# A decoder trunk's mixer: the delta rule's chain moved ahead of the stick-breaking attention, its small products joined, and the output projection begun with the attention heads

## The chip, the cores and the metric

The kernel runs on one core of one Trainium2 chip. The core has five engines that run side by side and wait for each other through semaphores: TensorE (PE in the profile, with PEld for its weight loads), VectorE (DVE), ScalarE (ACT), GpSimd (POOL) and SyncE (SP), which issues the DMAs. The metric is the device time of one execution in microseconds; smaller is better.

## What is computed

Two layers of a decoder trunk on 512 tokens of width 1024, all in fp32. Each layer does:

```python
h = layer_norm(alpha*h + 0.5*swiglu(h, ffa_w_in, ffa_w_out))
h = layer_norm(alpha*h + hybrid_mixer(h))
h = layer_norm(alpha*h + 0.5*swiglu(h, ffb_w_in, ffb_w_out))
h = h + sigmoid(h @ ple_w_gate) * (p @ ple_w_proj)

def hybrid_mixer(h):                       # cut
    proj = h @ w_in
    gq, gk, gv, gz, ga, gb, sq, sk, sv, mq, mkv = split(proj)
    o_gdn = gated_deltanet(gq, gk, gv, gz, ga, gb)       # 8 heads, chunks of 64
    o_sb  = stick_breaking_attention(sq, sk, sv)         # 4 heads
    o_mla = mla_attention(...)                           # 4 heads, low-rank q and kv
    return concatenate([o_gdn, o_sb, o_mla]) @ w_o
```

The gated delta rule solves, for each chunk of 64 tokens and each head, a unit lower triangular system for two right-hand sides, the scaled values (u) and the scaled keys (w), and then carries a 64 x 64 state from chunk to chunk.

## The kernel before

Every large product is made of three products of split operands (high and low part, fp32r), so one weight block of 128 rows is three matmuls, at L408 to L410 (helper mm3) or L414 to L416 (mm2, the feed-forward). Weights come by DMA on SP into three raw buffers, ACT makes the high part (L78), POOL or DVE the low part (L80), and the class Weights keeps three blocks ahead.

The program is written as steps whose order is the string "order" in OPT (lines 31 to 38); a planner that simulates the engines turns this order of emission into each engine's queue, with earlier steps taking precedence. The steps of the mixer (L620), by their names in the string:

- gates_in, gates, decays: the two gates and the matrices of decays, EA (strictly lower) and EU.
- k0..k3, q0..q3, v0..v3 (in_kq L841, in_values L863): a weight tile of 128 columns, 24 matmuls of 512 columns, a convolution over four tokens on DVE, a silu on POOL, ACT and DVE. v also transposes and scales by token into Vt (L871).
- si0..si3 (L905) and st (stick L1078; st03 is head pair 0, key tile 3): projections and steps of the stick-breaking attention. A step holds a PSUM bank of pair pb or pc while ACT, DVE and POOL compute its weights.
- scales, pr (products L875): K K^T and K Q^T for each token tile (L883), times EA and EU on DVE (L887).
- inv0, inv1, inv2, in2, in3 (L920 to L1007): the inverse of each chunk's triangular matrix. DVE eliminates blocks of 16 (L945, L946), then PE joins 16 to 32 (L970, L976, L978) and 32 to 64 (L992, L1003) with very small products.
- lat_in, lw, lh (latent_heads L754): latent projection, its weights, and the heads of each token tile.
- keys (L1010): the keys transposed by token, copied by DVE from PSUM into K (L1015). dm and dq: decays on keys' and queries' places.
- uw0..uw3 (u_w L1017): for token tile t, EA times V (L1022), ACT copies to Vt; POOL scales EA by cw2 (L647, helper by_token); EA times K (L1029), ACT copies to EA; POOL scales K by kd (L647 again).
- mv0..mv3 (moves L1042): products of w, K, EU and u (L1050, L1061, L1067). sc0..sc3 (scan L1113): the states from chunk to chunk, L1127 and DVE's addition L1128, then the output, L1132 and L1136. Its two PSUM tiles are the pair pb.
- gz0, gz1 (in_gz L1152): the output gate, GZ, 256 columns of weights at a time. on, go: a norm of the scan's output on DVE, and the gate times it on POOL (L1163).
- la00..la13 (latent L801; la02 is head pair 0, query tile 2), lo: softmax attention of the latent heads; pair 0 takes PSUM banks pc, pair 1 pb. Its buffers for weights lie in MW, SVM and SQK. mxa: the sticks' output split into MXh and MXl.

After the steps, the gates' product is transposed (L1198) and split into MGh and MGl, and the output projection runs: "out" gives the order of four weight blocks of 256 rows each; blocks 0 and 1 are the delta rule's half (MG), 2 the sticks' and 3 the latents' quarter (MX). The first 512 output columns open with the first two blocks for all four token tiles and close with the other two; then come the other 512 columns, and the norm (ln_finish L308), whose gain and bias ln_load (L295) loads into the tiles lng and lnb. These two tiles also hold the inverse's work. Large buffers are "units" (128 x 2048 fp32) out of a pool of 13, taken and given back as their readers finish; slabs of 512 columns come from a pool of four.

## Time and profile before

| | us |
|---|---|
| median of 3 runs | 2305.54 |
| lowest, highest | 2303.86, 2311.72 |
| profiled execution, its own time | 2302.08 |
| its span, first to last instruction | 2300.35 |
| PE busy (share of the span) | 2249.1 (98%) |
| DVE, ACT, POOL busy | 1297.9, 1058.7, 792.6 |

The first layer's mixer runs from about 364 us to 744 us, the second's from about 1507 to 1890. The rest is feed-forward, the embedding's step and the norms. In a view by stretches, a stretch in which PE's busy time equals its length had no standstill; since matmuls overlap and their ends are modelled, that is not yet PE at its peak, and the granted clock (1.00 is 2.4 GHz, 0.50 is 1.2 GHz) has to be read beside it. "issue" as a releaser means that the profile shows nothing that the engine waited for.

### The profile page before, as it was taken

How to read it: one execution, taken by the hardware profiler on the slowest of the kernel's cores; microseconds unless marked ns; L12 is line 12 of the kernel's file. 1: busy time of each engine (PE TensorE's matmuls, PEld its weight loads, DVE VectorE, ACT ScalarE, POOL GpSimd, SP SyncE). 2: the span in 40 equal slices, each digit the busy share in tenths (PEclk: the TensorE clock that was granted, in tenths of full speed). 3: DMA queues.
4: the chain of work that ended last, by engine and by line, in shares of the span. 5: the costliest groups of instructions: out<-in, count | busy, mean ns of one | idle time of the engine just before them, and what ended most of it. 6: DMA issues, size and time to landing. Idle time of an engine off the chain costs nothing.

```text
span 2300.3 us, 41397 instructions
## 1 busy us (share of the span) xinstructions
PE 2249.1 (98%) x17362; PEld 1997.8 (87%) x17362; DVE 1297.9 (56%) x2012; ACT 1058.7 (46%) x1751; POOL 792.6 (34%) x443
## 2 busy tenths in 40 slices
...
PEclk9999999998989999999999999999999899999999
...
GB/s 184 111 102 92 107 124 64 59 38 61 38 21 83 102 104 99 106 106 110 101 83 111 111 83 110 111 72 51 37 80 27 13 83 119 100 103 95 108 101 65
DMA packets 186795, 199.94 MB, mean 87 GB/s; under 512 B 10128, under 2 KB 151536, under 8 KB 186608
## 3 DMA queue, kind: packets, MB, share of 16 engines
...
## 4 chain that ended last, share of the span: by engine, by line
PE 95%; DVE 2%; POOL 1%; ACT 1%; issue 1%; DMA 0%; POOLq 0%; DVEq 0%; ACTq 0%
PE pi L408 6%; PE pi L409 6%; PE pi L410 6%; PE pc L414 4%; PE pc L416 4%; PE pc L415 4%; PE pa L416 3%; PE pa L414 3%; PE pa L415 3%; PE pb L416 3%; PE pb L415 3%; PE pb L414 3%; PE pc L410 3%; PE pb L410 3%; PE pb L408 3%; PE pc L409 3%
## 5 line engine op out<-in xcount | busy, mean ns | idle before, releaser
L80 POOL TENSOR_TENSOR wlo<-wraw,whi 128x1024 fp32r<-128x1024 f32 (+3 forms) x154 | 317.6, 2072 | 368.3 <-ACT whi L78 361.2
L78 ACT CAST whi<-wraw 128x1024 fp32r<-128x1024 f32 (+3 forms) x146 | 150.2, 1031 | 317.9 <-PE pa L410 144.7
L100 POOL TENSOR_TENSOR wlo<-wq,whi 128x1024 fp32r<-128x1024 f32 x40 | 99.6, 2490 | 371.8 <-ACT whi L99 368.6
L99 ACT CAST whi<-wq 128x1024 fp32r<-128x1024 f32 x116 | 121.8, 1050 | 128.2 <-issue 37.1
L100 POOL TENSOR_TENSOR wlo<-wraw,whi 128x1024 fp32r<-128x1024 f32 x32 | 83.1, 2597 | 232.6 <-ACT whi L99 184.4
L80 POOL TENSOR_TENSOR w<-wraw,w 128x1024 fp32r<-128x1024 f32 (+1 forms) x55 | 114.2, 2095 | 77.0 <-ACT w L78 76.7
L100 DVE TENSOR_TENSOR wlo<-wq,whi 128x1024 fp32r<-128x1024 f32 x76 | 95.1, 1252 | 79.8 <-ACT whi L99 79.8
L99 ACT CAST whi<-wraw 128x1024 fp32r<-128x1024 f32 x84 | 88.1, 1049 | 102.6 <-issue 25.5
L99 ACT CAST whi<-s 128x1024 fp32r<-128x1024 f32 x80 | 84.0, 1050 | 74.3 <-PE pc L415 34.3
L410 PE MATMUL pi<-x,wlo 128*128 128x512 f32 x256 | 104.2, 407 | 1.5 <-issue 1.5
L409 PE MATMUL pi<-x,whi 128*128 128x512 f32 x256 | 104.0, 406 | 0.0
L408 PE MATMUL pi<-x,whi 128*128 128x512 f32 x256 | 103.7, 405 | 0.0
L100 DVE TENSOR_TENSOR wlo<-wraw,whi 128x1024 fp32r<-128x1024 f32 x52 | 63.4, 1219 | 70.9 <-ACT whi L99 70.9
L100 DVE TENSOR_TENSOR wlo<-s,whi 128x1024 fp32r<-128x1024 f32 x80 | 97.0, 1213 | 0.2 <-ACT whi L99 0.2
L305 DVE SCALAR_TENSOR_TENSOR h<-h,pi 128x512 f32<-128x512 f32 x12 | 8.2, 687 | 146.6 <-PE pi L410 146.6
L414 PE MATMUL pi<-x,whi 128*128 128x256 f32 x320 | 90.6, 283 | 0.0
L415 PE MATMUL pi<-x,whi 128*128 128x256 f32 x320 | 90.6, 283 | 0.0
L416 PE MATMUL pi<-x,wlo 128*128 128x256 f32 x320 | 90.6, 283 | 0.0
L414 PE MATMUL pa<-t,whi 128*128 128x256 f32 x320 | 90.6, 283 | 0.0
L415 PE MATMUL pa<-t,whi 128*128 128x256 f32 x320 | 90.6, 283 | 0.0
L416 PE MATMUL pa<-t,wlo 128*128 128x256 f32 x320 | 90.6, 283 | 0.0
L414 PE MATMUL pc<-t,whi 128*128 128x256 f32 x320 | 90.6, 283 | 0.0
...
## 6 DMA issues: line engine op xcount, KB each, us to landing
...
```

The source lines that it names most:

```text
L78: self.nc.scalar.copy(hi[:, :width], raw[:, :width])
L80: (eng or self.nc.gpsimd).tensor_tensor(out=lo[:, c], in0=raw[:, c], in1=hi[:, c].bitcast(F32), op=ALU.subtract)
L99: nc.scalar.copy(hi, q[name])
L100: eng(name).tensor_tensor(out=lo, in0=q[name], in1=hi.bitcast(F32), op=ALU.subtract)
L305: V.scalar_tensor_tensor(out=hs, in0=hs, scalar=scale, in1=ps, op0=ALU.mult, op1=ALU.add)
L408: T.matmul(ps, ah, bh, start=first, stop=False)
L409: T.matmul(ps, ah, bl, start=False, stop=False)
L410: T.matmul(ps, al, bh, start=False, stop=last)
L414: T.matmul(dst, ah, bhl[:, 0], start=first, stop=False, skip_group_check=True)
L415: T.matmul(dst, ah, bhl[:, 1], start=False, stop=False, skip_group_check=True)
L416: T.matmul(dst, al, bhl[:, 0], start=False, stop=last, skip_group_check=True)
```

## The change

Both layers change in the same way.

- Order: the inverse (inv0 to in3) now follows the products of keys directly, behind st03, st02 and st01; si3, si1, st00, the steps of the second stick pair, the values and the latent projection come behind it. The latent projection is four steps (lat0 to lat3) in place of one. Scans and latents alternate by token tile (lo0 sc0, lo1 sc1, ...), the norms and gates come last.
- Values and keys: V becomes two units, VA and VB, two token tiles each; VK[t] holds values in its first row and scaled keys in its second. The values' scaling is two DVE operations in place of one.
- keys transposes by token tile; DVE scales out of PSUM twice, by cw2 into VK and by kd into K. The copies of K (c_K) and POOL's scalings of EA and K (by_EA, by_K) go.
- u_w: EA times values and scaled keys in one product of 128 columns, in two banks of four heads, and two ACT copies into VK, u in the place of the values and w in that of the keys. EA is no longer overwritten.
- Latent attention keeps its weights in the tile "x" that held the transposed input, in place of MW, SVM and SQK, with two places by token tile.
- GZ is no unit any more; the gates lie in the tiles lnb and lng.
- dq's two short operands are slabs in place of rows of LO.
- Output projection: blocks in the order 3, 2, 1, 0, the first two emitted ahead of the gates' transposes; their four banks are two of pi and two of pc in place of pi and pa. ln_load stands behind the transposes.

```diff
-    {"order": "gates_in gates q1 si3 si0 k0 k3 si1 decays si2 q2 st03 st02 k1 st01 q3 k2 st00 q0 scales pr2 pr0 st13 st12 st11 st10 pr3 lw pr1 inv0 inv1 inv2 v1 v0 lat_in in2 v3 v2 keys dm lh0 in3 lh3 dq lh2 qs lh1 uw0 mv0 uw1 mv1 uw2 mv2 uw3 mv3 gz0 gz1 la00 la10 lo0 la01 la11 lo1 mxa sc0 sc1 sc2 sc3 la02 la12 lo2 on0 go0 on1 go1 on2 go2 on3 go3 la03 la13 lo3",
-     "units": "MXl SQK EA KS SPb LO K KT KQ1 GZ MXh KQ0 SVM QT V EU MW MGh MGl SPa IA",
-     "out": (2, 1, 0, 3),
+    {"order": "gates_in gates q1 k0 si0 k3 si2 q2 decays k1 st03 q3 st02 k2 st01 q0 scales pr2 pr0 pr3 pr1 inv0 inv1 inv2 in2 in3 st00 si3 si1 v1 st13 v0 st12 v2 st11 v3 st10 lw lat0 lat1 lat2 lat3 keys dm dq lh0 lh1 uw0 mv0 uw1 mv1 gz0 lh2 qs uw2 mv2 gz1 lh3 uw3 mv3 la00 la10 lo0 sc0 la01 la11 lo1 sc1 mxa la02 la12 lo2 sc2 la03 la13 lo3 sc3 on0 go0 on1 go1 on2 go2 on3 go3",
+     "units": "MXl SQK EA KS SPb LO K KT KQ1 MXh KQ0 SVM QT VA VB EU MW MGh MGl SPa IA",
+     "out": (3, 2, 1, 0),
...
@@ -674,7 +671,8 @@
         EA, EU = U["EA"], U["EU"]
         SQK, SPa, SPb = U["SQK"], U["SPa"], U["SPb"]
         KQ = [U["KQ0"], U["KQ1"]]
-        KS, LO, Vt = U["KS"], U["LO"], U["V"]
+        KS, LO = U["KS"], U["LO"]
+        VK = [U[n][:, i:i + 2, :] for n in ("VA", "VB") for i in (0, 2)]
         KT, K, QT, MW = U["KT"], U["K"], U["QT"], U["MW"]
         gab = small("gab", 64)
         g3 = gab.rearrange("p (t c) -> p t c", t=NT)
...
@@ -734,12 +732,13 @@
                 EN["EUm"].tensor_tensor(out=ev, in0=ev, in1=tri_u.unsqueeze(1).broadcast_to([P, 8, 64]), op=ALU.mult)
 
 
-        def in_latent():
-            ws = [W.next() for _ in range(4)]
-            for t in range(NT):
-                ps = ibank()
-                tok_tile(ps[:, 0:416], t, ws, 416, 2)
-                CP["kt"](KT[:, t, 0:416], ps[:, 0:416])
+        lat_ws = []
+
+        def in_latent(t):
+            lat_ws.extend(W.next() for _ in range(0 if lat_ws else 4))
+            ps = ibank()
+            tok_tile(ps[:, 0:416], t, lat_ws, 416, 2)
+            CP["kt"](KT[:, t, 0:416], ps[:, 0:416])
 
         wuq = SQK[:, 2:4, :].rearrange("p a b -> p (a b)")
         wukv = SVM[:, 0, :]
...
@@ -796,9 +795,12 @@
                 CP["QKT"](dst[0:96, t, :], pp[0:96, :])
 
 
-        lo = {}
+
+        lo, old = {}, []
 
         def latent(h2, qt):
+            if not old:
+                old.append(xp.tile([P, 2, KD, S], F32, tag="x", name=nm("old")).rearrange("p a b s -> p (a b) s"))
             N = (qt + 1) * P
             if qt not in lo:
                 lo[qt] = slab("lo", 256)
...
@@ -809,7 +811,7 @@
                 T.matmul(s[:, qt * P:N], id_r, caus, start=False, stop=True)
                 mn, su = small("mx", 1, F32, 4), small("su", 1, F32, 4)
                 V.tensor_reduce(out=mn, in_=s[:, :N], op=ALU.min, axis=AX.X)
-                p_, pT = (MW[:, hp, :N], MW[:, 2 + hp, :N]) if h2 == 0 else (SVM[:, hp, :N], SQK[:, 2 + hp, :N])
+                p_, pT = (old[0][:, (h2 * 2 + qt % 2) * 4 + 2 * i + hp, :N] for i in range(2))
                 act(p_, s[:, :N], AF.Exp, scale=-1.0, bias=mn, accum_out=su)
                 V.reciprocal(su, su)
                 for kt in range(qt + 1):
...
@@ -868,8 +870,10 @@
                 pv = bank()
                 for t in range(NT):
                     T.transpose(pv[:, t * P:(t + 1) * P], y[:, t * P:(t + 1) * P], ident)
-                V.tensor_tensor(out=Vt[:, :, ct * P:(ct + 1) * P].rearrange("p t (h d) -> p t h d", h=2), in0=pv.rearrange("p (t h d) -> p t h d", t=NT, h=2),
-                                in1=th(brk)[:, :, 2 * ct:2 * ct + 2].unsqueeze(3).broadcast_to([P, NT, 2, 64]), op=ALU.mult)
+                for i, n in enumerate(("VA", "VB")):
+                    ts_ = slice(2 * i, 2 * i + 2)
+                    V.tensor_tensor(out=U[n][:, 0::2, ct * P:(ct + 1) * P].rearrange("p t (h d) -> p t h d", h=2), in0=pv.rearrange("p (t h d) -> p t h d", t=NT, h=2)[:, ts_],
+                                    in1=th(brk)[:, ts_, 2 * ct:2 * ct + 2].unsqueeze(3).broadcast_to([P, 2, 2, 64]), op=ALU.mult)
 
 
         def products(t):
...
@@ -891,8 +895,7 @@
             pt = bank()
             for t in range(NT):
                 T.transpose(pt[0:8, t * P:(t + 1) * P], th(egc)[:, t, :], ident)
-            eh, el = LO[:, 2, :], LO[:, 3, :]
-            sel = tp.tile([P, 512], F32R, tag="t", name=nm("sel"))
+            eh, el, sel = (tp.tile([P, 512], F32R, tag="t", name=nm(n)) for n in ("eh", "el", "sel"))
             EN["sel"].tensor_copy(sel[0:8, :].rearrange("p (h c) -> p h c", h=8), ident[0:8, 0:8].unsqueeze(2).broadcast_to([8, 8, 64]))
             split_from_psum(eh[0:8, :], el[0:8, :], pt[0:8, :])
             for h2 in range(4):
...
@@ -1008,27 +1011,21 @@
 
 
         def keys():
-            for ct in range(4):
+            for t in range(NT):
                 pk = bank()
-                for t in range(NT):
-                    T.transpose(pk[:, t * P:(t + 1) * P], kq(ct, 0)[:, t * P:(t + 1) * P], ident)
-                CP["K"](K[:, :, ct * P:(ct + 1) * P], pk.rearrange("p (t c) -> p t c", t=NT))
+                for ct in range(4):
+                    T.transpose(pk[:, ct * P:(ct + 1) * P], kq(ct, 0)[:, t * P:(t + 1) * P], ident)
+                by_token(V, VK[t][:, 1, :], pk, cw2, t)
+                by_token(V, K[:, t, :], pk, kd, t)
 
         def u_w(t):
-            pu = bank()
-            for hh in range(8):
-                for cp in range(2):
-                    R = slice(cp * 64, cp * 64 + 64)
-                    T.matmul(pu[R, hh * 64:(hh + 1) * 64], EA[R, t, hh * 64:(hh + 1) * 64], Vt[R, t, hh * 64:(hh + 1) * 64], start=True, stop=True)
-            CP["u"](Vt[:, t, :], pu)
-            by_token(EN["by_EA"], EA[:, t, :], EA[:, t, :], cw2, t)
-            pw = bank()
-            for hh in range(8):
-                for cp in range(2):
-                    R = slice(cp * 64, cp * 64 + 64)
-                    T.matmul(pw[R, hh * 64:(hh + 1) * 64], EA[R, t, hh * 64:(hh + 1) * 64], K[R, t, hh * 64:(hh + 1) * 64], start=True, stop=True)
-            CP["w"](EA[:, t, :], pw)
-            by_token(EN["by_K"], K[:, t, :], K[:, t, :], kd, t)
+            for i in range(2):
+                pu = bank()
+                for hh in range(4):
+                    for cp in range(2):
+                        R, c = slice(cp * 64, cp * 64 + 64), slice(i * 256 + hh * 64, i * 256 + (hh + 1) * 64)
+                        T.matmul(pu[R, hh * P:(hh + 1) * P], EA[R, t, c], VK[t][R, :, c], start=True, stop=True)
+                CP["w" if i else "u"](VK[t][:, :, i * 256:(i + 1) * 256].rearrange("p w (h d) -> p h w d", h=4), pu.rearrange("p (h w d) -> p h w d", h=4, w=2))
...
@@ -1047,7 +1044,7 @@
                     R = slice(cp * 64, cp * 64 + 64)
                     Rh, c = slice(hp * 64, hp * 64 + 64), slice(hh * 64, (hh + 1) * 64)
                     for w_, rhs in ((0, K), (1, EU)):
-                        T.matmul(pa[cp][Rh, w_ * 256 + h2 * 64:w_ * 256 + (h2 + 1) * 64], EA[R, t, c], rhs[R, t, c], start=True, stop=True)
+                        T.matmul(pa[cp][Rh, w_ * 256 + h2 * 64:w_ * 256 + (h2 + 1) * 64], VK[t][R, 1, c], rhs[R, t, c], start=True, stop=True)
             for cp in range(2):
                 c0 = t * P + cp * 64
                 for i in range(2):
...
@@ -1058,14 +1055,14 @@
                 pb = bank()
                 for hh in range(8):
                     h2, hp = hh // 2, hh % 2
-                    T.matmul(pb[hp * 64:hp * 64 + 64, h2 * 64:(h2 + 1) * 64], K[R, t, hh * 64:(hh + 1) * 64], Vt[R, t, hh * 64:(hh + 1) * 64], start=True, stop=True)
+                    T.matmul(pb[hp * 64:hp * 64 + 64, h2 * 64:(h2 + 1) * 64], K[R, t, hh * 64:(hh + 1) * 64], VK[t][R, 0, hh * 64:(hh + 1) * 64], start=True, stop=True)
                 CP["o"](SB[:, t, cp * 256:(cp + 1) * 256], pb[:, 0:256])
             pr_ = bank()
             for hh in range(8):
                 for cp in range(2):
                     R = slice(cp * 64, cp * 64 + 64)
-                    T.matmul(pr_[R, hh * 64:(hh + 1) * 64], EU[R, t, hh * 64:(hh + 1) * 64], Vt[R, t, hh * 64:(hh + 1) * 64], start=True, stop=True)
-            CP["o"](Vt[:, t, :], pr_)
+                    T.matmul(pr_[R, hh * 64:(hh + 1) * 64], EU[R, t, hh * 64:(hh + 1) * 64], VK[t][R, 0, hh * 64:(hh + 1) * 64], start=True, stop=True)
+            CP["o"](VK[t][:, 0, :], pr_)
 
 
         spa, spb, swf = (u.rearrange("p a b -> p (a b)") for u in (SPa, SPb, SVM[:, 2:4, :]))
...
@@ -1132,11 +1129,11 @@
                         T.matmul(po[hp][R, h2 * 64:(h2 + 1) * 64], kq(h2, 1)[Rh, c0:c0 + 64], old[Rh, h2 * 64:(h2 + 1) * 64], start=True, stop=True)
             R = slice(0 if t else 64, P)
             for hp in range(2):
-                o = Vt[R, t, :].rearrange(HP, h2=4, hp=2)[:, hp]
+                o = VK[t][R, 0, :].rearrange(HP, h2=4, hp=2)[:, hp]
                 V.tensor_tensor(out=o, in0=o, in1=heads(po[hp][R, 0:256], 4), op=ALU.add)
 
         def scan_norm(t):
-            o = Vt[:, t, :]
+            o = VK[t][:, 0, :]
             sq = slab("osq")
             act(sq, o, AF.Square)
             os_ = small("os", 8, F32, 2)
...
@@ -1147,20 +1144,25 @@
             V.tensor_tensor(out=heads(o), in0=heads(o), in1=of.unsqueeze(2).broadcast_to([P, 8, 64]), op=ALU.mult)
 
 
-        GZ = U["GZ"]
+        GZ = []
+
+        def gz(t):
+            if not GZ:
+                GZ.extend(x.rearrange("p (t c) -> p t c", t=2)[:, i, :] for x in (lnp.tile([P, 1024], F32, tag=n, name=nm("gz")) for n in ("lnb", "lng")) for i in range(2))
+            return GZ[t]
 
         def in_gz(n):
             ws = [W.next() for _ in range(2)]
             for t in range(NT):
                 ps = ibank()
                 tok_tile(ps[:, 0:256], t, ws, 256, 4)
-                CP["gz"](GZ[:, t, n * 256:(n + 1) * 256], ps[:, 0:256])
+                CP["gz"](gz(t)[:, n * 256:(n + 1) * 256], ps[:, 0:256])
                 if n == 1:
-                    silu(GZ[:, t, :], slab("e"))
-                    EN["gnw"].tensor_tensor(out=heads(GZ[:, t, :]), in0=heads(GZ[:, t, :]), in1=gnw.unsqueeze(1).broadcast_to([P, 8, 64]), op=ALU.mult)
+                    silu(gz(t), slab("e"))
+                    EN["gnw"].tensor_tensor(out=heads(gz(t)), in0=heads(gz(t)), in1=gnw.unsqueeze(1).broadcast_to([P, 8, 64]), op=ALU.mult)
 
         def gate_out(t):
-            EN["gout"].tensor_tensor(out=GZ[:, t, :], in0=GZ[:, t, :], in1=Vt[:, t, :], op=ALU.mult)
+            EN["gout"].tensor_tensor(out=gz(t), in0=gz(t), in1=VK[t][:, 0, :], op=ALU.mult)
 
         MXh, MXl, MGh, MGl = (U[n] for n in ("MXh", "MXl", "MGh", "MGl"))
...
@@ -1170,7 +1172,7 @@
                 EN["mxlo"].tensor_tensor(out=MXl[:, k, :], in0=SQK[:, k, :], in1=MXh[:, k, :].bitcast(F32), op=ALU.subtract)
 
         steps = {"gates_in": in_gates, "gates": gates, "decays": decays, "scales": scales, "qs": q_scales, "dq": decayed_queries,
-                 "lat_in": in_latent, "lw": latent_weights, "in2": inverse32, "in3": inverse64, "keys": keys, "gz0": lambda: in_gz(0), "gz1": lambda: in_gz(1),
+                 "lw": latent_weights, "in2": inverse32, "in3": inverse64, "keys": keys, "gz0": lambda: in_gz(0), "gz1": lambda: in_gz(1),
                  "mxa": lambda: split_heads(0), "inv0": inverse, "dm": decay_matrix, "inv1": eliminate, "inv2": turned}
         for t in range(NT):
             steps[f"k{t}"] = lambda t=t: in_kq(0, t)
...
@@ -1190,16 +1193,6 @@
                 steps[f"la{h2}{t}"] = lambda h2=h2, t=t: latent(h2, t)
         for st in opt["order"].split():
             steps[st]()
-        regroup("silu_and_others")
-
-        for t in range(NT):
-            pp = bank()
-            for ct in range(4):
-                T.transpose(pp[:, ct * P:(ct + 1) * P], GZ[:, t, ct * P:(ct + 1) * P], ident)
-            split_from_psum(MGh[:, :, t * P:(t + 1) * P], MGl[:, :, t * P:(t + 1) * P], pp.rearrange("p (c s) -> p c s", c=4))
-
-
-        ln_load(l, 1)
 
         def mm_o(ps, t, u, w, first, last):
             for kk in range(2):
...
@@ -1209,16 +1202,25 @@
                 mm3(ps, Mh[:, k % 4, ts_], Ml[:, k % 4, ts_], w[0][:, kk * 512:(kk + 1) * 512], w[1][:, kk * 512:(kk + 1) * 512], first and kk == 0, last and kk == 1)
 
         order = opt["out"]
-        ps0 = banks4()
+        ps0 = [ibank(), ibank(), one(True), one(True)]
         ws = [W.next() for _ in range(4)]
         for t in range(NT):
             for i in range(2):
                 mm_o(ps0[t], t, order[i], ws[i], i == 0, False)
+        regroup("silu_and_others")
+
+        for t in range(NT):
+            pp = bank()
+            for ct in range(4):
+                T.transpose(pp[:, ct * P:(ct + 1) * P], gz(t)[:, ct * P:(ct + 1) * P], ident)
+            split_from_psum(MGh[:, :, t * P:(t + 1) * P], MGl[:, :, t * P:(t + 1) * P], pp.rearrange("p (c s) -> p c s", c=4))
+
+        ln_load(l, 1)
         for t in range(NT):
             for i in range(2, 4):
                 mm_o(ps0[t], t, order[i], ws[i], False, i == 3)
             ln_half(t, 0, ps0[t], ALPHA)
-        pb = banks() + banks(True)
+        pb = banks() + [bank(), bank()]
         ws = [W.next() for _ in range(4)]
         new_xT(True)
         for t in range(NT):
```

## Rows read from the trace of the kernel before

**Rows 1.** The page: busy time per engine, and granted clock by slice
```profile
PE 2249.1 (98%) x17362; PEld 1997.8 (87%) x17362; DVE 1297.9 (56%) x2012; ACT 1058.7 (46%) x1751; POOL 792.6 (34%) x443
...
PEclk9999999998989999999999999999999899999999
```

**Rows 2.** Stretches, first layer's mixer: length, busy per engine, PEclk, DMA share, GB/s
```profile
540.00:580.00 40.00, 34.52 (x998) 30.25 (x996) 17.95 (x27) 11.16 (x20) 17.19 (x12) 0.79 0.23 72
580.00:655.00 75.00, 66.66 (x1003) 55.16 (x1003) 25.95 (x89) 37.47 (x92) 33.92 (x30) 0.91 0.13 41
655.00:700.00 45.00, 38.73 (x398) 31.50 (x395) 29.44 (x110) 21.16 (x58) 5.50 (x6) 0.92 0.01 1
700.00:743.70 43.70, 43.70 (x208) 36.12 (x207) 21.81 (x40) 14.61 (x21) 23.40 (x17) 1.00 0.33 99
```

**Rows 3.** The same view: second layer's mixer, and a stretch of 512-column products
```profile
1680.00:1720.00 40.00, 35.52 (x1013) 31.57 (x1012) 19.58 (x27) 16.92 (x29) 19.95 (x12) 0.87 0.27 83
1720.00:1800.00 80.00, 72.01 (x1030) 58.59 (x1030) 28.79 (x92) 37.53 (x93) 38.53 (x32) 0.89 0.13 41
1800.00:1845.00 45.00, 39.92 (x385) 31.56 (x381) 30.08 (x110) 20.02 (x57) 5.17 (x5) 0.89 0.01 1
...
1000.00:1080.00 80.00, 80.00 (x359) 66.19 (x358) 11.16 (x21) 19.89 (x22) 42.60 (x19) 1.00 0.39 118
```

**Rows 4.** Waits of PE, whole span: us in total, times, longest
```profile
PE pa L976 <- issue: 6.0, 4, 1.8
PE pb L1050 <- POOL K L647: 5.5, 3, 3.1
...
PE pa L1029 <- POOL EA L647: 4.4, 3, 2.0
PE pb L808 <- DVE V L1136: 3.8, 2, 2.3
...
PE pa L970 <- issue: 1.8, 1, 1.8
```

**Rows 5.** Chain of waits, last round of u_w: start us, us, what
```profile
646.19 0.96 PE pa L1022 x32
...
647.22 1.05 POOL EA L647
...
648.32 1.17 PE pa L1029 x32
...
649.56 1.05 POOL K L647
...
650.65 1.20 PE pb L1050 x58
```

**Rows 6.** Chain of waits, products of one token tile
```profile
513.18 1.51 PE pa L883 x16
```

**Rows 7.** DVE by form, mixer: xcount | busy us, mean ns | idle before
```profile
L871 DVE TENSOR_TENSOR V<-pa,brk 128x512 f32<-128x512 f32 x4 | 2.8, 689 | 0.8 <-PE pa L870 0.8
```

**Rows 8.** Stretches, instructions of L408 alone: length, PE, PEld busy, PEclk, DMA, GB/s
```profile
540.00:580.00 40.00, 9.79 (x25) 5.95 (x24) 0.79 0.23 72
...
655.00:700.00 45.00, 1.26 (x3) 0.57 (x3) 0.92 0.01 1
...
1680.00:1720.00 40.00, 12.44 (x35) 7.27 (x35) 0.87 0.27 83
```

**Rows 9.** The norm's loads: timeline, landing, first use, last gate transposes, SP's wait
```profile
578.22 0.34 SPq L298 DMA_DIRECT2D lng<-in_ln_g_dram  x1
...
DMA to landing us min/median/max: 3.4/3.5/3.8
...
729.37 0.74 DVE L319 SCALAR_TENSOR_TENSOR h<-h,ln_mv,lng 128x512 f32<-128x512 f32 x1
...
711.89 0.44 PE pa L1198 x4
...
SPq L62 <- PE pc L410: 21.4, 1, 21.4
```

13 lines of the change are left out of this document (6 added, 7 removed), and 6 rows, old and new, of the table OPT.

## The prediction

> **What bounds the kernel now.** I began with the busy shares and the row of slices: TensorE (PE) is busy 98% of the span, VectorE (DVE) 56%, ScalarE (ACT) 46%, GpSimd (POOL) 34% [rows 1]. The kernel is bound by PE as a whole, so a microsecond can only come from stretches in which PE stands still, from stretches in which it runs at the lower clock, or from PE work that goes away. The row of the granted clock shows where to look: it reads 8 in slices 10, 12, 32 alone, of 57.5 us each, which lie in the second halves of the two layers' mixers [rows 1]. The stretches give it in numbers. From 540 us to 700 us (first layer) PE's busy time falls short by 5.5, 8.3 and 6.3 us, from 1680 to 1845 us (second) by 4.5, 8.0 and 5.1 us, 37.7 us together; before and after it is full [rows 2, 3]. In the same stretches the mean granted clock is 0.79, 0.91 and 0.92, then 0.87, 0.89 and 0.89 [rows 2, 3]. As the clock has two levels, 2.4 and 1.2 GHz, a mean of 0.79 over 40 us says 2 x 0.21 x 40 = 16.8 us at the low one; all six add up to 75 us. What PE did before: small products with waits between, never a run of large ones. Third, the waits of PE by releaser: 6.0 and 1.8 us are "issue" inside the inverse's tiny products (L976, L970), 5.5 us POOL's scaling of K, 4.4 us POOL's scaling of EA, 3.8 us the latents' scores behind a scan's addition [rows 4]. So the prize is some 38 us of standstill and a part of 75 us at half speed, out of 2305; the feed-forward stages, which are most of the time, are untouched.
>
> The profiled execution took 2302.1 us with a span of 2300.3, 1.8 us lying around it; the median of the runs shown is 2305.5, 3.4 above. I sum against the profiled execution and add 3.4.
>
> **The change, part by part.**
>
> *Small products in one piece, keys scaled out of PSUM.* Now a round t of u_w and moves runs: 32 records of EA times V (0.96 us), POOL scales EA (1.05), 32 records of EA times K (1.17), POOL scales K (1.05), then the products of moves (L1050) [rows 5]. From the first product to L1050 that is 650.65 - 646.19 = 4.46 us, and the last round shows it bare, with no other work between. After the change the scaled keys lie beside the values, one set of products makes both halves, two ACT copies follow, and moves can begin: both POOL steps leave the chain. What is new in it: 32 records of 128 columns in place of 64 of 64. The trace has no such product. Its nearest rows are L1022, where products of the two 64-row halves alternate and a record of 64 columns takes 0.96/32 = 30 ns, and L883, 128 columns but all on one half, 1.51/16 = 94 ns [rows 5, 6]. Old: 0.96 + 1.17 = 2.1 us a round [rows 5]. New: 32 x 30 = 1.0 us at the least, 32 x 94 = 3.0 at the most, so -1.2 to +0.9 us a round, -9 to +7 over eight. I take 0: the columns are the same in number, and the halves alternate as in L1022.
> Here L1022 shows products of both halves of the rows going into one bank at 30 ns a record, against 47 for as many columns in L883 [rows 5, 6]. The Trainium skill, TensorEngine Tiling (Array Packing), section Restrictions and Gotchas, says that different row tiles cannot use one PSUM bank at the same time. By that the new, longer pieces would go one after the other, at the upper end, 7 us worse; the trace speaks against it.
> Of the 4.46 us then remain 2.1 for the products and about 0.6 for the copy. A round that has other PE work to fill it gains nothing, since PE never waited; what is sure is in the waits, 5.5 + 4.4 = 9.9 us [rows 4]. Against that, in about three uncovered rounds the copy (0.6 us) is now what PE waits for: 1.8. Net 8 us. The low clock takes 2 x 0.09 x 75 = 13.5 and 2 x 0.11 x 80 = 17.6 us in this stage [rows 2, 3]; without the POOL pauses I expect a tenth of that back, 3 us. **Rounds: -11 us**, between 0 (another engine late in POOL's place) and -20.
> DVE pays: eight scalings out of PSUM a layer, at the 0.69 us of the values' scaling 5.5 us [rows 7], less the four copies of K that go. DVE is busy 18 of 40 and 26 of 75 us there [rows 2]; the cover is its own slack, and the price without it at most 2 x 5.5 = 11 us. ACT keeps two copies a round. POOL loses eight scalings a layer that stood in its queue among gate and weight work.
>
> *The chain ahead of the sticks.* inv0 to in3 move in the hand-written order from behind the sticks, v and latent projections to just behind the products of keys; si3, si1, v0 to v3, half of the sticks and lat0 to lat3 come behind, and so are there to fill PE while DVE eliminates. No work is added. The issue gaps (7.8 us) belong to the tiny products and stay [rows 4]; of the 10.0 us of standstill in the two stretches 2.2 remain to be won. The clock stood low for 16.8 and 10.4 us [rows 2, 3]; a weight product is three instructions on three lines, of which L408 alone has 25 and 35 there [rows 8], so some 75 and 105; at the cadence of a full stretch, 80 us for 359 or 0.223 us [rows 3], they are 40 us of the 80. So half of 27.2 us at half speed is real work, and half of that, 6.8 us, to be won. **Inverse: -5 us**, between 0 and -9. The queue that it is moved past is DVE's: convolutions and the sticks' softplus now stand behind the elimination, and cost nothing while weight products feed PE. One limit: there are 13 units, and SQK, KS, SPa, SPb, LO, SVM, KQ0, KQ1, EA, EU, IA and the two new VA, VB fill them at the first v; the latent projection cannot land (KT) until the sticks have let go. It is fill for the later steps then, not for the inverse.
>
> *Scans between latents, output projection begun with the heads.* The stretch 655-700 holds only 3 weight products on L408, so some 9 on the three lines [rows 8]; PE lacks 6.3 us there and 5.1 in the second layer's [rows 2, 3]. After the change the first two weight blocks belong to the sticks and latents, ready before the scans' norms: 48 products x 0.223 = 10.7 us a layer [rows 3] that can stand where PE now waits for the norms on DVE and the gates on POOL. They are not saved, they are moved; the gain is the standstill that they fill, 11.4 us less the 3.8 us of waits that belong to the banks that scans and latents share [rows 4]. **End: -8 us**, between -14 (with the clock) and +11 (second rival).
>
> *Gates in the LN tiles.* The gates now lie in lng and lnb, so the loads of the next norm, issued at 578.2 us today, landing 3.5 us later and wanted at 729.4, must wait for the last transposes, 711.9 in today's time [rows 9]. That leaves 17 us for two loads of 3.5: free. The wait stands on SP's queue; behind it are the feed-forward's weights, wanted after 743.7, where the mixer ends. **0 us**, or the third rival.
>
> **Sum:** -11 - 5 - 8 = -24: 2302.1 - 24 = 2278.1 for the profiled execution, 2281.5 for the median. I forecast 2281 us.
>
> **The rivals.**
> First, *the whole gap closes*: with the chain ahead, rounds and tail find fill everywhere. The standstill without issue is 29.9 us, of which the terms take 8 + 7.6; 14 more go. If PE computed for 60% of the 75 us at low clock, running them at 2.4 GHz gives 22 us, of which the terms hold 8; 14 more: 2253 us. For it: every PE step of si, v and lat is there to fill. Against: the tiny products of the inverse and the scans are the longest low stretch, and stay.
> Second, *the change doesn't do what it says*: the order is only a priority for the planner, and at the end the scans ask for both pb banks, which the second latent pair needs too. Today the four scans run in a row and the latents wait twice, 3.8 us [rows 4]. Alternating them makes four hand-overs of 1.9 us where there was one, 3 x 1.9 x 2 = 11.4 us more, and the end's 8 us are not won: 2300. If the full unit pool also keeps the inverse bare, 2305. I say 2303.
> Third, *slower*: SP issues in order. One load of today's queue stands 21.4 us until a product frees its place and goes at 740.3 [rows 9]. If the norm's loads are queued behind that one, ln_finish waits from 729.4 to 744 (with the landing), 15 us, and then two tiles must be normalised in the open, two operations like L319's 0.74 us each: 18 us a layer, 2281 + 36 = 2317. It decides from about 17 us of delay behind the last transposes.
> Fourth, *serial pieces*, the two halves of the new products not overlapping in a bank: +7 us, 2288. For it speaks nothing in the rows, against it L1022's 30 ns. The page of the Trainium skill named above would give this time.
>
> **How the numbers follow.** Forecast 0.48 (own range 2266 to 2295), gap closes 0.18, no effect 0.17, slower 0.12, serial pieces 0.05. The range reaches from 2248 (most of the first rival) to 2306 (most of the second); the lowest part of the first, some of the second and all of the third stay out, about 0.2. Differences within 0.3%, 7 us, are about what a measurement of this kernel cannot tell from none. Faster: 0.47 + 0.18 + 0.03 + 0.05 = 0.73; same: 0.01 + 0.12 + 0.01 = 0.14; slower: 0.02 + 0.11 = 0.13.
>
> **What would show it.** Rounds right: no POOL line among the releasers of L1050, and u_w's records halved, at 30 to 50 ns each; at 94 the pieces are serial. Inverse right: weight products of si and v between its records, and more of them in that stretch; wrong: the clock still at 0.8 there and only "issue" and DVE as releasers. End right: some forty weight products on MX ahead of the transposes of the gates; wrong: scores of the latents waiting for L1136 oftener than now. Gates right: the norm's first operation waits for DVE, not for the load; wrong: a DMA as its releaser. The forecast as a whole is wrong if the stages outside the mixers change, since nothing of them is touched, or if filled stretches keep the low clock, since then half of my gain was never there.

## The result and the profile of the changed kernel

The changed kernel takes 2324.2 us (median of 4 runs, 2321.0 to 2332.7) against 2305.1 for the kernel before beside it: a ratio of 1.0098, 95% interval 1.0080 to 1.0115. It is slower by about 1%; I had forecast 2281 and given "slower" 0.13. The profiled execution has a span of 2321.7 us, 21.4 above that of before.

The page of the changed kernel, busy time and the row of the granted clock (against [rows 1]):

```profile
PE 2263.2 (97%) x17106; PEld 2007.8 (86%) x17106; DVE 1324.9 (57%) x2028; ACT 1059.1 (46%) x1751; POOL 776.0 (33%) x427
...
PEclk9999999997999999999999999999979899999999
```

POOL lost work, DVE gained some, and the dips of the clock are not gone but gathered and deeper: 7 in slices 10 and 30, 58 us each, where the inverse now lies, and 8 in slice 32. The view by stretches says what is in them (against [rows 2, 3]; columns: stretch, its length, PE, PEld, DVE, ACT, POOL busy, granted clock, share of the DMA engines, GB/s):

```profile
500.00:520.00 20.00, 14.80 (x212) 13.01 (x210) 17.99 (x41) 7.53 (x13) 6.35 (x6) 1.00 0.19 54
520.00:545.00 25.00, 19.42 (x759) 17.90 (x760) 7.18 (x11) 4.79 (x9) 3.72 (x4) 0.54 0.02 4
545.00:580.00 35.00, 31.86 (x115) 17.73 (x115) 15.08 (x36) 22.43 (x52) 9.46 (x10) 0.84 0.05 16
580.00:655.00 75.00, 72.62 (x913) 60.36 (x911) 30.62 (x81) 40.01 (x90) 36.15 (x25) 1.00 0.19 55
655.00:700.00 45.00, 43.97 (x399) 36.81 (x400) 23.43 (x88) 21.39 (x63) 11.18 (x9) 0.89 0.17 48
700.00:747.40 47.40, 42.82 (x240) 34.28 (x239) 34.24 (x74) 16.90 (x27) 19.36 (x13) 0.96 0.22 67
...
1660.00:1680.00 20.00, 12.71 (x364) 11.66 (x364) 11.85 (x28) 6.29 (x11) 2.80 (x4) 0.89 0.12 33
1680.00:1700.00 20.00, 17.34 (x597) 15.38 (x589) 7.78 (x12) 4.08 (x7) 3.38 (x3) 0.50 0.02 5
```

Three things are to be seen. From 580 to 655, the stretch of the rounds, PE lacks 2.4 us where it lacked 8.3, at clock 1.00 for 0.91: what I forecast, and more. From 655 to 700 it lacks 1.0 for 6.3. But the inverse, now at 518 to 546, has the clock at 0.54, and it brought its standstill along: 5.2 us from 500 to 520, 5.6 from 520 to 545. And the end, full before, lacks 4.6 us. In the second layer the inverse's stretch lies wholly at the low level, 0.50.

The longest waits of PE (against [rows 4]; columns: who waits, for whom, us in total, times, longest):

```profile
PE pc L794 <- DVE MW L790: 7.5, 3, 3.2
PE pa L263 <- DVE h L320: 7.0, 2, 3.5
PE pi L408 <- DVE y L841: 5.8, 2, 2.9
PE pa L973 <- issue: 4.7, 2, 2.5
```

The POOL lines of [rows 4] are gone; DVE has taken their place, in the latent heads (L794), at the norm ahead of the next transposes (L263) and in the convolutions (L841).

Why the inverse is so bare shows in L408 alone, one of the three lines of a weight product, by the same view (PE's busy time and count; kernel before, then after; against [rows 8]):

```profile
480.00:520.00 40.00, 5.53 (x15) 1.00 0.15 41
520.00:545.00 25.00, 11.21 (x31) 0.97 0.29 78
545.00:580.00 35.00, 9.40 (x24) 0.78 0.16 53
580.00:620.00 40.00, 8.71 (x31) 0.96 0.15 48
```

```profile
480.00:520.00 40.00, 14.54 (x38) 1.00 0.18 51
520.00:545.00 25.00, 0.00 (x0) 0.54 0.02 4
545.00:580.00 35.00, 0.60 (x2) 0.84 0.05 16
580.00:620.00 40.00, 14.60 (x48) 1.00 0.21 61
```

Their number is about the same, 101 and 88, but they lie elsewhere: before they are spread over the whole stretch, after there are 38, 0, 2, 48. The last products of si and v ran until 503 us, and those of the latent projection's first two token tiles (the ones of 416 columns) from 505 to 517, while DVE eliminated. Then none came for 62 us:

```profile
517.10 0.35 PE L410 MATMUL pi<-whi,x 128*128 128x416 f32 x1
578.63 0.92 ACT L741 COPY KT<-pi 128x416 f32<-128x416 f32 x2 [0.51 <-PE pb L1100]
579.18 0.45 PE L408 MATMUL pi<-whi,x 128*128 128x416 f32 x1
```

Every weight product of an input projection goes into one of the two banks of pi (helper ibank). The two token tiles' results lay in both of them until ACT could copy them out at 578.6, when KT had its unit, and the next weight product began right behind that copy. In the second layer it is the same: the products end at 1671.2, the copy starts at 1731.1. In the kernel before the copies follow within 2 us of their products, the first at 521.2:

```profile
L742 ACT COPY KT<-pi x4: 501/506/516, 521.2 to 535.6; 128x416 f32<-128x416 f32 x4
```

Nor did earliness buy anything: the inverse's last copy starts at 545.3 (581.7 before), but the first product of u_w starts at 609.0 us (588.4 before), since u_w also needs the values, the keys and PE. The inverse was finished 63 us too early.

### The profile page after: what moved, and what is told of

It is laid out like the page before. It is cut to its first block, busy times and chain, and to the rows that moved or that the text cites. A ratio compares the mean times of both kernels' runs of the same rounds, so it can differ in the third digit from the quotient of the medians.

```text
span 2321.7 us, 40906 instructions
## 1 busy us (share of the span) xinstructions
PE 2263.2 (97%) x17106; PEld 2007.8 (86%) x17106; DVE 1324.9 (57%) x2028; ACT 1059.1 (46%) x1751; POOL 776.0 (33%) x427
## 4 chain that ended last, share of the span: by engine, by line
PE 91%; DVE 4%; ACT 2%; issue 1%; DMA 1%; POOL 0%; SPq 0%; DVEq 0%; ACTq 0%; POOLq 0%
PE pi L408 6%; PE pi L410 6%; PE pi L409 6%; PE pc L414 4%; PE pc L415 4%; PE pc L416 4%; PE pa L415 3%; PE pa L414 3%; PE pa L416 3%; PE pb L416 3%; PE pb L414 3%; PE pb L415 3%; PE pb L408 3%; PE pb L410 3%; PE pb L409 3%; PE pc L410 3%
## 5 line engine op out<-in xcount | busy, mean ns | idle before, releaser
L408 PE MATMUL pi<-x,whi 128*128 128x512 f32 x256 | 104.1, 407 | 2.5 <-DVE KQ L841 2.5
L410 PE MATMUL pi<-x,wlo 128*128 128x512 f32 x256 | 102.6, 401 | 0.0
L414 PE MATMUL pa<-x,whi 128*128 128x256 f32 x320 | 90.7, 283 | 0.0
L414 PE MATMUL pc<-t,whi 128*128 128x256 f32 x320 | 90.6, 283 | 0.0
L415 PE MATMUL pc<-t,whi 128*128 128x256 f32 x320 | 90.6, 283 | 0.0
L416 PE MATMUL pc<-t,wlo 128*128 128x256 f32 x320 | 90.6, 283 | 0.0
L414 PE MATMUL pc<-x,whi 128*128 128x256 f32 x320 | 90.6, 283 | 0.0
L415 PE MATMUL pc<-x,whi 128*128 128x256 f32 x320 | 90.6, 283 | 0.0
L416 PE MATMUL pc<-x,wlo 128*128 128x256 f32 x320 | 90.6, 283 | 0.0
L414 PE MATMUL pb<-x,whi 128*128 128x256 f32 x320 | 90.6, 283 | 0.0
```

The source lines that it names most:

```text
L408: T.matmul(ps, ah, bh, start=first, stop=False)
L410: T.matmul(ps, al, bh, start=False, stop=last)
L414: T.matmul(dst, ah, bhl[:, 0], start=first, stop=False, skip_group_check=True)
L415: T.matmul(dst, ah, bhl[:, 1], start=False, stop=False, skip_group_check=True)
L416: T.matmul(dst, al, bhl[:, 0], start=False, stop=last, skip_group_check=True)
```

## The experiments

Each row is one kernel, with its ratio to the kernel before on the same chip (2301.6 to 2306.5 us there; medians of different rows therefore compare to some 3 us). "Undone" means as in the kernel before.

| run | what it is | median us | ratio, 95% interval |
|---|---|---|---|
| (the change) | | 2324.2 | 1.0098 (1.0080 to 1.0115) |
| e4_head | first part of the order (up to gz1) undone | 2286.2 | 0.9924 (0.9899 to 0.9949) |
| e1_banks | banks of the second 512 columns undone | 2312.5 | 1.0048 (1.0028 to 1.0067) |
| e5_head_banks | both undone | 2268.3 | 0.9847 (0.9823 to 0.9871) |
| e2_ln_unit | norm's gain and bias in a unit | 2347.2 | 1.0169 (1.0123 to 1.0215) |
| e3_tail | end of the order undone | 2324.3 | 1.0088 (1.0054 to 1.0122) |
| e8_head_banks_tail | e5 with the end undone | 2277.8 | 0.9881 (0.9852 to 0.9910) |
| e6_rounds | kernel before with the rounds alone | 2279.8 | 0.9893 (0.9869 to 0.9918) |
| e7_inv_ahead | e5 with the inverse moved ahead | 2322.4 | 1.0081 (1.0059 to 1.0104) |
| e11_before_inv | kernel before with the inverse moved ahead | 2336.3 | 1.0149 (1.0119 to 1.0179) |
| e9_mq | e1, homes of latent projection and gates exchanged | 2312.0 | 1.0038 (1.0014 to 1.0063) |
| e10_mq_head | e5 with the same exchange | 2320.1 | 1.0086 (1.0053 to 1.0119) |
| e12_split | e5 with the pieces of u_w apart | 2270.1 | 0.9851 (0.9822 to 0.9881) |
| e13_fill | the change, useless products in the inverse | 2359.6 | 1.0232 (1.0192 to 1.0271) |
| e14_swap | e5, the gates' two tiles exchanged | 2267.1 | 0.9826 (0.9793 to 0.9859) |

Sums by function, used below, are mine from the trace: the time from the start of each product to the start of the next, added up over both layers.

**e1_banks.**

```diff
-        pb = banks() + [bank(), bank()]
+        pb = banks() + banks(True)
```

> The changed kernel with one thing undone: the second 512 output columns of the projection take the banks pb, pb, pc, pc of the kernel before in place of pb, pb, pa, pa. Theory 'banks': pa is also what the transposes of the next stage's input take, so the 24 products of token tile 3 (5.4 us at 0.223) are pushed behind the feed-forward's first products and the transposes of tiles 0 and 1 wait bare for the norm (3.5 us each layer). Undone: L263's waits (7.0 us in the two layers) go, and the time falls by 6 to 9 us, to 2315 to 2318. Theory 'load': the norm is late by itself, behind its gain, which was issued at 728.2 us; then the banks change nothing, 2322 to 2325. If pc is late too (the first half still holds it), the time rises, by 5 us.

2312.5 us, 11.7 less, more than I expected, and the transposes' waits for the norm are gone: L263's sum falls from 35.8 to 27.2 us, while the norm's gain is loaded no earlier (730.9 us). The banks were the cause, not the load. In the changed kernel t=2's products of the second half cannot start until transposes have given pa back, and t=3's run at 754 to 760, inside the feed-forward.

**e2_ln_unit.**

```diff
-        gt = lnp.tile([P, D], F32, tag="lng", name=nm("lng"))
-        bt = lnp.tile([P, D], F32, tag="lnb", name=nm("lnb"))
+        if i == 1:
+            gb = unit("lnu").rearrange("p a b -> p (a b)")
+            gt, bt = gb[:, 0:D], gb[:, D:2 * D]
...
```

> The changed kernel, with gain and bias of the mixer's norm loaded into a large buffer of their own (a unit) in place of lng and lnb, where the gates lie. Theory 'load' (the third rival of the prediction, in small): the two loads no longer wait for the last transposes (lng issued at 728.2, first used at 732.0), the norm starts some 3 us earlier in each layer and the gain is 5 to 8 us, 2316 to 2319. Theory 'banks' or 'late chain': the norm waits for the products anyway and the load is covered; 2322 to 2325. By the third rival's full price (18 us a layer) it would be 2288.

None of these: 23 us slower. The loads were early indeed, issued at 715.9, but PE's waits for the norm grew to 19.0 us and the sum of the feed-forward's products by 17.3. I take it that the unit which the loads occupied was missing elsewhere; no run shows that. For the load the run is inconclusive.

**e3_tail.**

```diff
-  ... la00 la10 lo0 sc0 la01 la11 lo1 sc1 mxa la02 la12 lo2 sc2 la03 la13 lo3 sc3 on0 go0 ...
+  ... la00 la10 lo0 la01 la11 lo1 mxa sc0 sc1 sc2 sc3 la02 la12 lo2 on0 go0 ... la03 la13 lo3
```

> The changed kernel with the end of the order as before: the four scans in a row behind the latents of two tiles, norms and gates next, the latents of the last tile at the very end; projection, banks and storage stay as changed. Theory 'late chain': with scans between the latents the last scan's outputs come at 711.8 us (679.5 before), the last transposes of the gates at 727.5 (711.9 before), and this sets when the norm's gain can be loaded; undone, the end comes 6 to 10 us earlier in each layer, 2305 to 2312. Theory 'fill': alternating is what keeps the low clock away there (the stretch 680 to 700 has it at 1.00 with full PE, 0.83 and 15.0 us busy before); undone, 5 us a layer come back, and the two cancel or it is slower: 2322 to 2334.

No difference, the second theory's lower end. On this kernel the end's order hides behind its banks.

**e4_head.**

```diff
-  ... scales pr2 pr0 pr3 pr1 inv0 inv1 inv2 in2 in3 st00 si3 si1 v1 st13 v0 ... st10 lw lat0 ...
+  ... st00 q0 scales pr2 pr0 st13 st12 st11 st10 pr3 lw pr1 inv0 inv1 inv2 v1 v0 lat0 lat1 lat2 lat3 in2 v3 v2 ... in3 ...
```

> The changed kernel with the first part of the order as before: the inverse behind the sticks and between values, latent projection and heads; everything from the rounds on as changed. Theory 'spent fill': with the chain ahead, the weight products of the values and of the last si run while DVE eliminates (500 to 517 us), and 517 to 562 us holds no weight product at all, clock 0.55 and 0.60 in 520 to 560, so the small products of inverse and second stick pair run at the low level. Sums by function, both layers: stick +16.3, inverse +14.6, waits of weight products +8.3 us. Undone, 10 to 20 us come back: 2304 to 2314. Theory 'neutral' (the standstill was only moved, 12.7 us to 12.8): 2320 to 2328. By my prediction (chain ahead wins 5): 2329.

2286.2, 38.0 us less: twice the upper end of "spent fill", on its side. The function sums go back with it: stick 96.3 to 80.6, inverse32 33.3 to 23.8, weight products of L408 to L410 1001.4 to 997.8. So the rest of the change wins, and its first part turns that into a loss; e7 and e11 ask whether the inverse's move does it alone. The stretches of e4:

```profile
500.00:520.00 20.00, 20.00 (x117) 13.58 (x117) 10.08 (x23) 10.32 (x17) 5.36 (x5) 1.00 0.16 48
520.00:540.00 20.00, 20.00 (x100) 17.25 (x100) 14.90 (x44) 6.37 (x12) 4.00 (x2) 1.00 0.06 17
540.00:580.00 40.00, 33.52 (x963) 29.21 (x963) 17.53 (x30) 13.41 (x23) 16.30 (x11) 0.79 0.25 80
```

PE is full while DVE eliminates (520 to 540, DVE busy 14.9), and only the tiny products are left at the low clock.

**e5_head_banks** undoes e4's and e1's parts together.

> The changed kernel with two things undone: the first part of the order as before (2286.2 us alone) and the banks of the second 512 columns (11 to 12 us alone). Theory 'two places': the two losses lie in different stretches and add, so the time is 2274 to 2279. Theory 'one cover': with the first part as before the norm's waits are hidden otherwise and the banks bring less than 4: 2282 to 2286. In the profile L263's wait for the norm (9.6 us) goes, by both it must fall.

2268.3, below all theories: the losses lie in two places and more than add (17.9 us for the banks here, 11.7 alone). This version beats both kernels: 1.5% faster than before. Its waits of PE, longest first, hold no line for the norm any more:

```profile
PE pb L981 <- issue: 6.0, 4, 1.8
PE pa L263 <- DMA h<-in_x_dram: 4.7, 1, 4.7
PE pi L408 <- issue: 2.0, 1, 2.0
PE pa L1064 <- ACT IA L1059: 2.0, 1, 2.0
```

**e6_rounds** is the kernel before with only u_w, keys, VA and VB, and the storage that they need (gates in the norm's tiles, the latents' weights in x, the slabs of dq), changed; order, projection and banks undone.

> The part 'rounds' alone, with the storage that it needs: the whole order, the projection, its banks and its order of blocks as before; merged products of u_w, keys scaled out of PSUM by DVE, the gates in the norm's tiles and the latents' weights in the tile x as changed. By the prediction's term (rounds -11, gates in the norm's tiles 0): 2289 to 2293, and no POOL releaser for L1050's successor L1047. If the gates in the norm's tiles cost (loads behind the last transposes), 3 us a layer more: 2295. If the gain of 15 us that stood beside the old first part comes all from the end's order, rounds give nothing: 2300 to 2304. In u_w 256 records of 63 ns on the mean stand against 512 of 49 now: 9 us are to be won by them alone.

22.5 us less, twice the term. POOL is no releaser in the rounds any more. The stretches (against [rows 2, 3]):

```profile
580.00:655.00 75.00, 72.75 (x971) 60.24 (x967) 32.99 (x103) 41.93 (x110) 30.57 (x23) 0.97 0.10 30
...
1720.00:1800.00 80.00, 77.58 (x1092) 63.33 (x1091) 37.56 (x131) 44.12 (x117) 26.86 (x21) 1.00 0.08 28
```

The standstill fell by 6.1 and 5.6 us. At the low level there are now 2 x 0.03 x 75 = 4.5 us and none, where there were 13.5 and 17.6: 26.6 us went back to full speed, of which I had counted a tenth.

**e7_inv_ahead** moves one step in e5, **e11_before_inv** the same step in the kernel before:

```diff
-  ... pr2 pr0 st13 st12 st11 st10 pr3 lw pr1 inv0 inv1 inv2 v1 v0 lat0 ... in2 v3 v2 keys dm lh0 in3 lh3 ...
+  ... pr2 pr0 pr3 pr1 inv0 inv1 inv2 in2 in3 st13 st12 st11 st10 lw v1 v0 lat0 ... v3 v2 keys dm lh0 lh3 ...
```

> The run with first part and banks as before, and in it one step moved: inv0 to in3 directly behind the products of keys, ahead of the second pair's sticks, the values and the latent projection (in the changed kernel sticks, si and values were reordered too). Theory 'spent fill': the move by itself is the loss: the weight products that stand behind it (values, latent projection) come too late or too early for the tiny products, the clock there is at the low level again, and the time is 10 to 30 us above the run without the move, 2287 to 2305. Theory 'sticks': the loss belongs to the sticks' new places (stick was the largest sum, +16.3), and the move alone costs less than 5 us, 2274 to 2281. By the prediction it would win 5: 2271.

> The kernel before with one step of the change alone: inv0 to in3 directly behind the products of keys, ahead of the second pair's sticks, values and latent projection; no other edit. The prediction gave this step -5 us (0 to -9): 2297. Theory 'full pool / spent fill': the loss that the changed kernel had (38 us, and 54 on the run without its other orders) belongs to this step and needs none of the others: 2340 to 2360, with elimination bare (PE waits for L955's successor on DVE by some 15 us a layer) and the clock at 0.5 in the inverse. Theory 'interaction' (only with VA and VB as two units is the pool too small): 2295 to 2310.

54.0 us slower than e5, far above the range of "spent fill", and 34 slower than the kernel before (2302.7 beside it), a little under that of "full pool / spent fill". The move by itself makes the loss, with and without the other edits. On the better kernel it costs more alone than with the reordering that the change adds (54.0, against 44.2 from e5 to e1): there the last of v and half of the latent projection, reordered with it, covered most of the elimination. Kernel before with the move, its longest wait and its stretches:

```profile
PE pa L970 <- DVE IA L956: 30.1, 2, 15.0
```

```profile
500.00:520.00 20.00, 6.30 (x44) 5.30 (x40) 14.09 (x43) 2.73 (x4) 0.00 (x0) 0.70 0.00 0
520.00:540.00 20.00, 13.66 (x674) 12.67 (x676) 5.12 (x6) 3.87 (x7) 0.53 (x1) 0.50 0.02 4
```

PE stands 15.0 us in each layer until DVE has eliminated, then runs the tiny products at 1.2 GHz throughout. Weight products are still to come here, half of v among them, but the latent projection's first two token tiles are through at 506 us and keep both banks of pi until 527.3; the next weight product starts at 541.9. In e7 none comes between 507 and 572.8.

**e9_mq and e10_mq_head.** The latent projection's output waited in the changed kernel for a unit: KT is first written at 578.6 us, where the sticks have read theirs (522.6 in e5). Here it goes into the norm's two tiles (mq_ gives half of lnb or lng), and the gates into a unit.

```diff
-            CP["kt"](KT[:, t, 0:416], ps[:, 0:416])
+            CP["kt"](mq_(t)[:, 0:416], ps[:, 0:416])
...
         def gz(t):
...
-            return GZ[t]
+            return U["GZ"][:, t, :]
```

> The changed kernel with the banks of before (2312.5 us alone), its whole order as changed, and two homes exchanged: the output of the latent projection goes into the norm's tiles in place of the unit KT, the gates into a unit. In the changed kernel KT was first written at 578.6 us, when the last stick had read its unit SPa, so the latent projection could not stand beside inverse and sticks; with the chain's order of before it was written at 522.6. Theory 'full pool' (the 13 units are what takes the fill away): the 96 products of the latent projection now lie before and among the second pair's sticks, the stretch 520 to 580 gets weight products and the high clock, and 15 to 25 us come back: 2288 to 2298. Theory 'serial chain' (DVE's elimination, the inverse and the sticks' chain through ACT and DVE now stand one behind the other, whatever fills them): less than 8 us, 2305 to 2313.

> The same exchange of homes on the run with the first part and the banks of before (2268.3 us), as the control: there KT came at 522.6 already. Also the norm's gain is no longer behind the gates' transposes (DVE waited 2.5 us for it). Theory 'full pool': nothing to win in the first part, 0 to 5 us from the norm's load: 2263 to 2269. If taking fill away ahead of the inverse hurts here too (the latent products would now run before the tiny products), 5 to 15 us slower: 2273 to 2283.

e9: 2312.0, as without the exchange (2312.5). The fill came earlier, but not into the inverse; L408 alone, by stretches:

```profile
480.00:520.00 40.00, 14.73 (x38) 0.96 0.14 41
520.00:545.00 25.00, 0.00 (x0) 0.51 0.02 5
545.00:580.00 35.00, 11.08 (x32) 0.96 0.20 65
580.00:620.00 40.00, 0.00 (x0) 0.87 0.10 31
```

The sticks have it now (against e1 their sum falls by 15.3 us), and the steps behind them miss it: latent heads +8.5, decayed queries +6.2, scans +3.4. The exchange did not make the room that I wanted: lng and lnb also hold the inverse's own work, so the latent projection cannot land in them (be copied out of PSUM) before the inverse is through (543.6 us), and the gates cannot land before their unit is free (633.0). Each time both banks of pi stay occupied, and no weight product runs from 517 to 545 us and from 575.5 to 634 us:

```profile
L746 ACT COPY mq<-pi x4: 490/495/507, 543.6 to 562.0; 128x416 f32<-128x416 f32 x4
L1160 ACT COPY GZ<-pi x3: 371/373/377, 633.0 to 637.4; 128x256 f32<-128x256 f32 x3
```

e10 lost 52 us against e5. Its latent products run when they do in e5 (first at 497.7 us, 494.6 there), but they land 42 us later (564.6 for 522.6), behind the inverse, and no weight product starts between 529 and 565.2. The picture is that of e11 (PE waits twice 8.7 us for L964, behind the elimination, and the clock is 0.50):

```profile
520.00:540.00 20.00, 11.26 (x89) 8.72 (x91) 16.74 (x47) 3.66 (x6) 0.32 (x1) 0.86 0.05 13
540.00:560.00 20.00, 13.94 (x708) 13.14 (x702) 5.89 (x8) 3.05 (x6) 0.53 (x1) 0.50 0.01 4
```

So the two runs do not refute "full pool": they moved the place at which a result waits to land, and the pause went with it. Nor do they refute "serial chain", whose range (2305 to 2313) e9's time fits.

**e8_head_banks_tail** is e5 with e3's edit.

> The run with first part and banks as before, and also the end of the order as before (scans in a row): only rounds, storage and the projection begun with the heads' half remain of the change. On the changed kernel this end made no difference (2324.3 against 2324.2). Theory 'neutral': 2274 to 2279 again. Theory 'late chain': with the banks right the last transposes set the end, and the earlier scans give 3 to 8 us more: 2268 to 2274. Theory 'fill': 3 to 8 us slower, 2280 to 2286, and the low clock in the scans' stretch again.

9.5 us slower than e5, and the clock of the whole run at 0.986 for 0.992: the relation is that of "fill", a little more than its 3 to 8 us, though all three were set from a level that e5 then undercut. With the banks right the alternation of scans and latents is worth it; the run stands 2 us from e6, so the projection's early start alone brought nothing that can be measured.

**e12_split.**

```diff
-                        T.matmul(pu[R, hh * P:(hh + 1) * P], EA[R, t, c], VK[t][R, :, c], start=True, stop=True)
+                        for w in range(2):
+                            T.matmul(pu[R, hh * P + w * 64:hh * P + (w + 1) * 64], EA[R, t, c], VK[t][R, w, c], start=True, stop=True)
```

> The run with the first part and the banks of before (2268.3 us), with the products of u_w in two pieces again: 512 records of 64 columns in place of 256 of 128, into the same banks and places, so that merging alone is undone and the keys stay scaled out of PSUM. My prediction gave the merging 0 (between -9 and +7). Theory 'columns' (what a piece costs goes by its columns; all the gain of u_w, 25.3 to 15.9 us, came from the missing POOL steps): the same within 3 us, 2266 to 2271, records of some 31 ns. Theory 'records' (each record has a price of its own, 49 ns for 64 columns against 62 for 128): 5 to 9 us slower, 2273 to 2278.

2270.1, within the interval the same: "columns". By elimination what won in the rounds is the missing POOL steps; the rest of e6's storage was not undone by itself.

**e13_fill.**

```diff
+        def fill(n, ps, src):
+            if n % 4 == 3 and n < 24:
+                T.matmul(ps[:, 384:512], ident, src, start=True, stop=True)
```

> The changed kernel (2324 us) with 22 products a layer more that compute nothing of use: between the inverse's tiny products one 128 x 128 x 128 product after every fourth of 32 groups, into a place of the same bank that is overwritten later. They cost 22 x 0.13 us or about 3 us a layer at the high clock, 6 in all. Theory 'the low clock is the loss' (granted 0.55 and 0.60 in 520 to 560, some 34 us at the low level in the first layer): larger products between keep the clock up, inverse32 and inverse64 (33.3 and 15.8 us) come back to 24 and 10, and the sticks behind them start at the high level: 2300 to 2316. Theory 'missing work' (PE waits for DVE, ACT and for itself in chains that nothing useful covers; the low clock is a companion): the time rises by the fillers' price, 2328 to 2336.

fill is called in all four loops of the inverse. 31 us slower by the ratios, 35 by the medians: above both theories. There were 24 such products a layer, not 22, each of two records, and I had priced one record at the high clock; by my sum they took 30.6 us, while the inverse's own products gave back 6.5. They did not bring the clock back either:

```profile
520.00:540.00 20.00, 18.28 (x585) 15.10 (x578) 4.45 (x7) 2.47 (x4) 1.49 (x1) 0.63 0.01 4
540.00:560.00 20.00, 20.00 (x254) 13.71 (x253) 4.59 (x9) 4.16 (x7) 1.89 (x2) 0.50 0.01 2
```

So the question is not settled by it: whether the same products at the high clock would lose as much was not tried, since no row here has them there. What it does show is that more activity of this kind is no remedy.

**e14_swap.**

```diff
- ... for n in ("lnb", "lng")) for i in range(2))
+ ... for n in ("lng", "lnb")) for i in range(2))
```

> The run with the first part and the banks of before (2268.3 us), with the gates' two tiles exchanged: the gates of token tiles 0 and 1 in lng, of 2 and 3 in lnb, so that the gain (needed first) can be loaded after the second transposes and only the bias waits for the last. In that run DVE waits for the gain, but PE waits for nothing at L263. Theory 'covered': the load is hidden behind the 48 products of token tiles 2 and 3, no change, 2265 to 2271. Theory 'third rival in small': each wait of DVE (2.5 us) is on the path, 3 to 5 us faster, 2263 to 2265.

2267.1 against 2268.3: covered. DVE waited at most 2.3 us for the bias, as it had for the gain, and PE did not wait for DVE's norm.

## Why the prediction was wrong, step by step

By medians the parts stand in this chain: before 2302.3, with the rounds alone 2279.8 (-22.5), with the end too 2286.2 (+6.4), with the chain ahead 2324.2 (+38.0). My terms were -11, -8 and -5.

*What bounds the kernel*: right. What moved lies in the mixers and their ends: the feed-forward ahead of the first mixer ends at 237.7 us (237.9 before), and that ahead of the second takes 228.7 us (228.8); only the feed-forward behind each mixer is 6 us longer, since the mixer's last products now run in it.

*Inverse, -5 us, between 0 and -9: the step that failed, in sign.* e11 gives this step +34 us on the very kernel for which I had priced it, e7 +54, and the first part of the order as a whole +38.0. What failed is the overlap: si, v, sticks and latent projection "are there to fill PE while DVE eliminates". They filled part of it (PE is busy 13.0 of the 17 us from 500 to 517), and nothing after it. What the runs show in its place is the pause without weight products, 62 us a layer in the changed kernel, while two results that could not land kept both banks of pi. I had half of this: I wrote that the latent projection "cannot land (KT) until the sticks have let go" and is "fill for the later steps then, not for the inverse", and gave a bare inverse 5 us, in the second rival. But its first two token tiles did run, and what they then kept from running I did not ask. A late landing goes with the loss in every kernel here: in the kernel before and the six that are faster (e4, e5, e6, e8, e12, e14) the two tiles' copies follow their products within 2 us, in the nine that are slower (the change, e1, e2, e3, e7, e9, e10, e11, e13) the first copy comes 21 to 77 us after the two tiles' last product.

In time, from e4 to the change (their profiles, 34.0 us apart in span): PE's standstill grows from 43.0 to 58.5 us, and its busy time by 18.5 us for the same work, with the time at the low level from 58.7 to 123.9 us. So somewhat less than half of the loss is standstill, and the rest is work that takes longer. Whether a moved inverse would win if the results could land was not tried: no run moves it and keeps the banks free. That leaves a rival open, the chain of DVE, ACT and PE by itself.

Two more things I left out. What the move uncovers: the fill had covered the tiny products (25 weight products on L408 between 540 and 580 [rows 8]), and the second pair's sticks had run between the products of keys at clock 1.00; now they run alone, at 0.84 from 545 to 580. And whether anyone wants the inverse earlier: u_w came 20.6 us later. The bound of 0 on the loss side had no reason behind it: that no PE work is added does not exclude that PE work loses its cover.

*Rounds, -11 (0 to -20): right, and too small.* POOL's releasers of the next step are gone. Both parts were mis-sized, the clock most: I took 8 us of standstill and 3 for a tenth of the 31 us at low speed in these stretches; e6 shows 11.7 us and 26.6 of the 31.1, and over its whole profile 12.1 us less standstill and 9.0 less busy time. The copy that I charged in POOL's place, 1.8 us, is not among the waits. A round's products took 2.0 us, as I put it:

```profile
646.83 1.96 PE L1027 MATMUL pa<-VB,EA 64*64 64x128 f32 x32
```

That is 61 ns a record between my bounds of 30 and 94, and merging is worth no more than the runs can tell, as I said (e12). *Serial pieces*, the fourth rival, fell with it: these records start in pairs, 6 ns apart, a pair every 109 ns, where L883's, all on one half, come singly at 109 ns. The Trainium skill, TensorEngine Tiling (Array Packing), section Restrictions and Gotchas, has it that different row tiles cannot use one PSUM bank at the same time; the records of the two halves here go into one bank, so the trace disagrees again.

*End, -8 (-14 to +11): the mechanism was right, a line of the diff was left out.* Some 36 products on MX ran at 670 to 700 us, ahead of the transposes of the gates, and the stretch 655 to 700 lost its standstill. But I did not cost the banks of the second 512 columns, where pa in place of pc puts 48 products, those of token tiles 2 and 3, and the transposes of the norm's output against each other. With the banks of before the end wins 11.5 us (e6 to e5), of which the alternation is 9.5; with those of the change it loses 6.4. The *second rival*, hand-overs between scans and latents, fell: alternating them gains.

*Gates in the norm's tiles, 0 us, or the third rival.* The mechanism is in the trace, small. The gain's tile in the changed kernel:

```profile
L319 DVE SCALAR_TENSOR_TENSOR h<-h,ln_mv,lng x2: 742/747/752, 732.0 to 737.0; 128x512 f32<-128x512 f32 x2
L298 SPq DMA_DIRECT2D lng<-in_ln_g_dram x1: 341/341/341, 728.2 to 728.2; - x1
...
  DVE h L319: 2.6, 1
```

The load left at 728.2, right behind the last transposes at 727.5, which had been at 711.9 [rows 9]; DVE waited 2.6 us, not 15. e14 shows it covered once the banks are right, so 0 was the right price there. The slower outcome came, then, but not from my slower rival; what happened stood as half a sentence in the second rival, an inverse that stays bare, and I had that end at 2305.

*DVE's price*: the scalings took 11.0 us and the copies that went 5.5, as I had it. But DVE's busy time rose by 27.0 us; much of the rest is operations of the same form and number that took longer (the latent heads' products with sin 11.6 us for 5.2). Why stays open; nothing above depends on it.

*The range* (2248 to 2306) had the chain's loss in no case. With that term at e11's +34 in place of -5 the same sum gives 2281.5 + 39 = 2320. That this lies near 2324 is luck: the rounds brought 11.5 us more than their term, and the end came out 14.4 us worse than its.
